# A channel shuffle on one core: where the small tile stands, and the last stores in halves

## Chip, core and metric

The kernel runs on one core of a Trainium2 chip. The metric is the device time of one execution in microseconds (us); lower is better.

## The reference

The input is a float32 tensor of 16 x 64 x 64 x 256 (67.1 MB). Each row of 256 channels is seen as 8 groups of 32; the two are transposed inside the row.

```python
x = x.reshape(batch, h, w, groups, channels_per_group)   # 8 groups of 32
x = x.transpose(0, 1, 2, 4, 3)
x = x.reshape(batch, h, w, c)
```

Nothing is computed. Every byte must be read once and written once: 134.2 MB in all.

## The kernel before

The 65,536 rows are cut into tiles. A tile of size q gives each of the 128 partitions q rows of 1 KB, which are contiguous in memory. So a tile of 24 is "24 KB per partition", 3 MB in all, and one load or store of it is 128 runs of 24 KB.

```python
_SIZES = [24] * 20 + [8, 24]      # rows of 1 KB per partition; sum 512
_BUFS = 8
_PIECE = 8
# ...
    for q in _SIZES:
        buf = pool.tile([P, biggest * c], F32, name="buf")
        nc.sync.dma_start(out=buf[:, : q * c], in_=rows(x_flat, first, q))
        for k in range(0, q, _PIECE):
            piece = buf[:, k * c : (k + _PIECE) * c]
            bounce = psum.tile([P, _PIECE * c], F32, name="bounce")
            nc.vector.tensor_copy(          # the shuffle, SBUF to PSUM
                out=bounce.rearrange("p (i j g) -> p i j g", j=CPG, g=G),
                in_=piece.rearrange("p (i g j) -> p i j g", g=G, j=CPG),
            )
            nc.scalar.copy(out=piece, in_=bounce)   # and back
        nc.scalar.dma_start(out=rows(out_flat, first, q), in_=buf[:, : q * c])
        first += P * q
```

SyncE (SP) issues the loads, VectorE (DVE) shuffles pieces of 8 KB into PSUM, ScalarE (ACT) copies them back over the piece, and ScalarE also issues the stores. Loads and stores share eight completion semaphores in turn (the trace shows eight numbers for all 44 DMAs). Before the change, each of the 36 DMAs that reuse one was issued only after the DMA that used it last had landed, 6 of them within 0.1 us. So the order of all DMAs, and not only buffers, decides who waits for whom.

## Time and profile before

| | before |
|---|---|
| time, median of the first 3 runs (317.38 to 317.92) | 317.67 us |
| span of the profile | 315.9 us |
| load queue and store queue, share of the 16 DMA engines' span | 49.9% + 49.4% |
| VectorE, ScalarE busy | 72%, 38% |
| last store: issue, landing | 302.46 us, 12.4 us later |

The first lines are from the profile page of the kernel before: the span, the rows of 40 slices (busy tenths of VectorE, ScalarE and the DMA engines, then GB/s), the two DMA queues (q1 loads, q10 stores) with packets, MB and share of 16 engines, and the chain of waits by engine.

```profile
span 315.9 us, 289 instructions
...
DVE  0699999959587685957008986999970299999900
ACT  0354455525252424330015416545500444555420
...
DMA  8999999999999999999999999999999999999997
GB/s 296 439 442 380 436 429 433 433 439 433 423 442 433 426 442 426 426 442 426 433 436 427 433 436 436 433 426 437 433 423 448 423 429 444 429 423 433 439 432 302
...
q1 hardware_dynamic: 3168, 67.11, 49.9%
q10 hardware_dynamic: 3168, 67.11, 49.4%
...
DVE 54%; another core or an unknown queue 23%; issue 8%; ACT 5%; DMA 3%; DVEq 1%; ACTq 0%
```

Read the DMA row first: 9 in 38 slices of 40, and the two queues together fill 99.3% of the engines' span. VectorE has two holes (0 in the middle, 02 near three quarters) that leave no mark in the DMA row. The chain of waits names VectorE for 54%. It follows releases backwards from the last instruction and does not know that a released DMA had to queue behind others.

These lines are from the timeline of the kernel before (start, duration, engine, line, operation): the start, one of the stops, and the end. ACTq is ScalarE's sequencer issuing a store, SPq is SyncE issuing loads.

```profile
0.73 3.06 SPq L50 DMA_DIRECT2D buf<-in_x_dram  x6
11.05 3.60 DVE L54 COPY bounce<-buf 128x2048 f32<-128x2048 f32 x1 [11.05 <-DMA buf<-in_x_dram]
...
248.38 0.34 ACTq L59 DMA_DIRECT2D out_dram<-buf  x1
248.81 3.63 ACT L58 COPY buf<-bounce 128x2048 f32<-128x2048 f32 x2 [19.19 <-DMA buf<-in_x_dram]
250.71 3.65 DVE L54 COPY bounce<-buf 128x2048 f32<-128x2048 f32 x1 [15.93 <-ACT buf L58]
...
297.01 1.86 ACT L58 COPY buf<-bounce 128x2048 f32<-128x2048 f32 x1 [1.69 <-DVE bounce L54]
300.57 1.86 ACT L58 COPY buf<-bounce 128x2048 f32<-128x2048 f32 x1 [1.69 <-DVE bounce L54]
302.46 0.34 ACTq L59 DMA_DIRECT2D out_dram<-buf  x1
```

Near 248 us ScalarE could not issue a store, because the semaphore it was to reuse belonged to a load that had not landed (by the semaphore records it landed at 248.3 us; the store went out at 248.38). Its copies stood behind that store for 19.19 us, and VectorE stood behind ScalarE for 15.93 us. The DMA engines had other work queued (from 220 to 252 us they moved 434 GB/s, at a busy share of 1.01), so this cost nothing.

The trace also has a record of every packet: start, duration, bytes, queue. A 24 KB packet takes 912 ns, an 8 KB packet 309 ns, a semaphore write 9 ns (medians). The page counts 16 DMA engines, and from 10 to 300 us 16 records were in progress for 93% of the time and 17 for nearly all of the rest, so I count each record on one of 16 engines.

### The profile page before, as it was taken

The page shows a single profiled execution, that of the slowest core. Times are in us where ns is not written, and L with a number is a line of the kernel's source. Part 1 is how long each engine was busy: PE and PEld are TensorE (multiplying, and loading weights), DVE is VectorE, ACT ScalarE, POOL GpSimd, SP SyncE. Part 2 cuts the span into 40 slices and gives each one's busy share as a digit, 9 for nine tenths or more (in the row PEclk, how much of TensorE's full clock was granted, in tenths as well). Part 3 has the DMA queues.
Part 4 walks back from the last instruction along what each step waited for, and adds up shares of the span by engine and source line. Part 5 has one row for each costly group of instructions (what it writes and reads, how often), then busy time and mean ns, then how long its engine had stood idle before and what let it go on. Part 6 is the DMA issues. An engine that isn't in the chain of part 4 may idle for free.

```text
span 315.9 us, 289 instructions
## 1 busy us (share of the span) xinstructions
DVE 227.9 (72%) x64; ACT 120.3 (38%) x65; POOL 0.2 (0%) x4
## 2 busy tenths in 40 slices
DVE  0699999959587685957008986999970299999900
ACT  0354455525252424330015416545500444555420
POOL 0000000000000000000000000000000000000000
DMA  8999999999999999999999999999999999999997
GB/s 296 439 442 380 436 429 433 433 439 433 423 442 433 426 442 426 426 442 426 433 436 427 433 436 436 433 426 437 433 423 448 423 429 444 429 423 433 439 432 302
DMA packets 6338, 134.24 MB, mean 425 GB/s; under 512 B 704, under 2 KB 704, under 8 KB 704
## 3 DMA queue, kind: packets, MB, share of 16 engines
q1 hardware_dynamic: 3168, 67.11, 49.9%
q10 hardware_dynamic: 3168, 67.11, 49.4%
q14 instruction: 2, 0.02, 0.0%
HBM read 67.11 MB, written 67.11 MB: 425 GB/s over the span
## 4 chain that ended last, share of the span: by engine, by line
DVE 54%; another core or an unknown queue 23%; issue 8%; ACT 5%; DMA 3%; DVEq 1%; ACTq 0%
DVE bounce L54 54%; ACT buf L58 5%; DMA buf<-in_x_dram 3%; DVEq L91 1%; ACTq L59 0%; DVEq L54 0%; ACTq L58 0%
## 5 line engine op out<-in xcount | busy, mean ns | idle before, releaser
L54 DVE COPY bounce<-buf 128x2048 f32<-128x2048 f32 x64 | 227.9, 3636 | 72.6 <-ACT buf L58 38.8
L58 ACT COPY buf<-bounce 128x2048 f32<-128x2048 f32 x64 | 119.0, 1866 | 171.1 <-DVE bounce L54 115.3
L58 ACT ACT_TABLE_LOAD x1 | 1.3, 1283 | 11.1 <-DMA buf<-in_x_dram 11.1
L77 POOL MEMSET const-bfloat16-1.0<- 128x1 bf16 x1 | 0.1, 102 | 0.0
L77 POOL MEMSET const-uint8-127<- 128x1 uint8 x1 | 0.1, 101 | 0.0
L77 POOL MEMSET const-float32-0.0<- 128x1 f32 x1 | 0.1, 99 | 0.2 <-issue 0.2
L77 POOL MEMSET const-float32-1.0<- 128x1 f32 x1 | 0.1, 98 | 0.0
## 6 DMA issues: line engine op xcount, KB each, us to landing
buf<-in_x_dram SPq DMA_DIRECT2D x21, 3072.0 KB, 58.4
out_dram<-buf ACTq DMA_DIRECT2D x21, 3072.0 KB, 24.2
buf<-in_x_dram SPq DMA_DIRECT2D x1, 1024.0 KB, 46.0
out_dram<-buf ACTq DMA_DIRECT2D x1, 1024.0 KB, 15.8
```

The costliest lines, as they stand in the source:

```text
L54: nc.vector.tensor_copy(out=bounce.rearrange("p (i j g) -> p i j g", j=CPG, g=G), in_=piece.rearrange("p (i g j) -> p i j g", g=G, j=CPG),)
L58: nc.scalar.copy(out=piece, in_=bounce)
L77: nc = _bacc.Bacc("TRN2", target_bir_lowering=False, num_devices=1)
L91: with _tile.TileContext(nc) as tc:
```

## The change

The intent: let VectorE start earlier by loading the 8 KB tile first, and give the end of the program finer stores. This makes 48 DMAs of 44.

```diff
-_SIZES = [24] * 20 + [8, 24]
+_SIZES = [8] + [24] * 21
...
+_HALVED = (18, 19, 20, 21)
...
-    for q in _SIZES:
+    for t, q in enumerate(_SIZES):
...
-        nc.scalar.dma_start(out=rows(out_flat, first, q), in_=buf[:, : q * c])
+        n = 2 if t in _HALVED else 1
+        for k in range(n):
+            cols = slice(k * q // n * c, (k + 1) * q // n * c)
+            nc.scalar.dma_start(
+                out=rows(out_flat, first, q)[:, cols], in_=buf[:, cols]
+            )
```

## The prediction

> **What bounds the kernel now.** The DMA engines. The queue table gives loads 49.9% and stores 49.4% of the 16 DMA engines' span of 315.9 us, 99.3% together; the slice row shows DMA at 9 in 38 of 40 slices, 425 GB/s over the span. [...] this trace's 24 KB packets take 912 ns each on one of 16 engines, 431 GB/s[...]. VectorE is 72% busy, ScalarE 38%. The chain of waits shows 54% VectorE, which misleads: the last store is issued at 302.46 us and lands 12.4 us later, although its own eight packets per engine need 7.3. It queues about 4 us behind earlier stores, so the engines don't run dry at the end.
>
> Budget per DMA engine: 336 packets of 24 KB x 0.912 + 16 of 8 KB x 0.309 + 44 semaphore writes x 0.009 = 311.8 us. First packet at 1.7 us, about 0.6 of slow first packets, 0.5 of stagger at the end: last packet at 314.6. Then 1.3 to the span's end, 1.8 more to the timed 317.67.
>
> **What the change does.**
> - Bytes, VectorE copies (64 x 3.64 us) and ScalarE copies (64 x 1.87): the same.
> - 8 KB tile first: VectorE's first copy starts near 6-7 us instead of 11.05, as the first landing needs a third of the bytes. But the DMA engines are full of loads then; an earlier first store only changes the mix. Worth 0.
> - The end: the last tile's stage is the same three VectorE pieces, 3.55 us apart. Worth 0.
> - Halves: ScalarE's order keeps all three copies of a tile ahead of both its stores, so the first half starts no earlier. Four more issues (0.34 us each, off the path); 32 packets of 24 KB per engine become 64 of 12 KB. From 309 ns for 8 KB and 912 for 24 KB I estimate 460 for 12 KB: 32 x 7.5 + 4 x 9 ns = +0.3 us.
> - Eight completion semaphores are shared by loads and stores in turn, so 48 DMAs shift who waits for whose landing (before: ScalarE's store near 248 us waited for a load, stopping VectorE 16 us). Stepping the new order through with the durations above (estimate), stalls move, several transfers stay queued throughout, and the last half store is issued near 301.7 us with some 5 us of earlier work ahead: never dry.
>
> [...]
>
> **Prediction: 317.9 us**, range 317.2 to 318.8. Faster by over 2%: 0.01; within 2%: 0.98; slower: 0.01.
>
> **What would show it.** Both queues again sum to 99%; DMA slices 9 throughout; first VectorE copy at 6-7 us; VectorE and ScalarE busy unchanged; span within 0.6 us of 315.9; eight half stores of 1536 KB, the last two issued within 0.4 us of each other near 302 us; ScalarE's waits for load landings in other places, but not at the very end.
>
> **What would make it wrong.** If semaphore sharing delays the last stores by over 4 us, the engines run dry and each further us counts fully. If 12 KB packets are slower than 460 ns, or half rows write slower, 1 us or more. If small first packets shorten the slow start, up to 0.6 us gained.

311.8 us of packets per engine, the first packet, slow packets, stagger and ends up to the timed 317.67, and 0.3 us for the halves come to 318.0; the forecast put it at 317.9.

## The result, and the profile after

| | before | after |
|---|---|---|
| time, median of 6 runs each | 317.63 us (317.38 to 317.92) | 317.57 us (317.47 to 317.98) |
| ratio, 95% interval | | 1.0 (0.9987 to 1.0013) |
| span | 315.9 us | 315.7 us |
| first VectorE copy | 11.05 us | 5.62 us |
| last store issued (after: its halves) | 302.46 us | 298.81 and 300.64 us |

A ratio here is the mean time of one kernel's fast runs over the mean of the other's fast runs of the same rounds, so it is not quite the ratio of the quoted medians.

The same lines of the page of the kernel after:

```profile
span 315.7 us, 295 instructions
...
DVE  2599979595959577695956049999904999999800
ACT  1245552442425252424330044555204554445500
...
DMA  7999999999999999999999999999999999999997
GB/s 317 403 414 409 442 445 420 433 445 436 414 445 439 411 445 442 408 445 445 406 442 445 408 442 445 420 436 442 431 420 442 436 420 439 439 417 423 433 430 330
...
q1 hardware_dynamic: 3168, 67.11, 49.8%
q10 hardware_dynamic: 3744, 67.11, 49.5%
...
DVE 45%; another core or an unknown queue 22%; DMA 14%; issue 6%; ACT 5%; DVEq 1%; SPq 1%; ACTq 1%
```

VectorE's row has moved: it starts in the first slice, and its holes stand elsewhere. The chain of waits has changed from 54% to 45% VectorE. The DMA row is still 9 between its outer slices and the queues sum to 99.3%. By this reading the DMA row sets the time; the experiments below test it.

The timeline of the kernel after, at its start, near 280 us and at its end:

```profile
5.62 3.60 DVE L56 COPY bounce<-buf 128x2048 f32<-128x2048 f32 x1 [5.62 <-DMA buf<-in_x_dram]
...
13.10 3.60 DVE L56 COPY bounce<-buf 128x2048 f32<-128x2048 f32 x1 [3.88 <-DMA buf<-in_x_dram]
...
276.48 1.87 ACT L60 COPY buf<-bounce 128x2048 f32<-128x2048 f32 x1 [1.69 <-DVE bounce L56]
276.54 5.92 ACTq L64 DMA_DIRECT2D out_dram<-buf  x2
282.50 3.63 ACT L60 COPY buf<-bounce 128x2048 f32<-128x2048 f32 x2 [4.16 <-DMA buf<-in_x_dram]
...
298.75 1.87 ACT L60 COPY buf<-bounce 128x2048 f32<-128x2048 f32 x1 [1.69 <-DVE bounce L56]
298.81 2.17 ACTq L64 DMA_DIRECT2D out_dram<-buf  x2
```

There are two things to see. VectorE starts early, but then waits 3.88 us for the second load. And at 298.81 the first half store is issued 0.06 us after the tile's last copy *started*, not after it ended: the first half needs only the first two pieces, and ScalarE's sequencer issued the DMA while the copy ran. These two pieces had been copied by 297.06 us already (the copy before started at 295.19 and took 1.87); what still held the half store was the third copy, which stands before it in ScalarE's order and had not started. (Three other tiles are stored in halves in this trace; their first halves were issued at 265.89, 276.54 and 288.15 us, each 0.06 or 0.07 us after the start of the tile's last copy.) The second half follows when that copy is done, 1.83 us later (the "x2" line merges the two: 2.17 us less the 0.34 us of one issue).

### The sum of the packets

To see differences far below 1% I added up the packet records of each trace, as a mean of the 16 DMA engines (sums over all packets, divided by 16). "Nominal" is every packet at the usual duration of its size. "Slow" is what packets took beyond that, before and after the change nearly all in the first 30 us. The records do not name the engine, so the other two are counted over all 16 together: "overlap" is the records in progress beyond 16 at a time, and "idle" is what is missing from 16, at the start (before 10 us), in between, and at the end (after 300 us). An engine that idles while another's records overlap would not be seen. Nominal + slow - overlap + idle is the time of the last packet, to within rounding of 0.01. All in us. The lower rows are experiments that follow. Each row is one profiled execution, and the runs of one kernel differ by 0.5 us and more, so tenths in this table describe that execution.

| kernel | DMAs | nominal | slow | overlap | idle start | idle between | idle end | last packet |
|---|---|---|---|---|---|---|---|---|
| before | 44 | 311.77 | 1.77 | 1.44 | 1.88 | 0.04 | 0.55 | 314.56 |
| after | 48 | 312.06 | 1.50 | 1.55 | 2.12 | 0.03 | 0.43 | 314.60 |
| small tile first alone | 44 | 311.77 | 1.43 | 1.44 | 2.17 | 0.06 | 0.29 | 314.28 |
| halves alone | 48 | 312.07 | 1.68 | 1.56 | 1.87 | 0.04 | 0.58 | 314.67 |
| all stores halved | 65 | 313.31 | 1.47 | 2.06 | 2.14 | 0.03 | 0.51 | 315.40 |
| 8 KB packets | 44 | 316.81 | 1.48 | 3.32 | 2.43 | 0.03 | 0.63 | 318.07 |
| 16, ten of 48, 16 | 24 | 310.17 | 1.97 | 0.71 | 2.05 | 0.04 | 0.97 | 314.49 |
| 8, ten of 48, 24 in halves | 26 | 310.31 | 1.67 | 0.76 | 2.11 | 0.04 | 0.48 | 313.85 |
| before, last tile late | 44 | 311.77 | 1.70 | 1.43 | 1.91 | 0.03 | 7.57 | 321.55 |
| small tile first, last tile late | 44 | 311.77 | 1.75 | 1.43 | 1.88 | 0.04 | 4.70 | 318.71 |
| after, last tile late | 48 | 312.06 | 1.49 | 1.54 | 2.13 | 0.04 | 4.11 | 318.29 |
| all stores in quarters | 107 | 316.37 | 7.73 | 3.13 | 2.35 | 7.16 | 10.27 | 340.76 |

Before and after differ by 0.29 in nominal, by 0.1 in overlap, and by 0.1 to 0.3 in the rest. "Idle between" is 0.04 of 290 us: the 16 engines together never run dry between 10 and 300 us.

### The profile page after: what moved, and what is told of

It is laid out like the page before. It is cut to its first block, busy times and chain, and to the rows that moved or that the text cites. A ratio compares the mean times of both kernels' runs of the same rounds, so it can differ in the third digit from the quotient of the medians.

```text
span 315.7 us, 295 instructions
## 1 busy us (share of the span) xinstructions
DVE 228.0 (72%) x64; ACT 120.3 (38%) x65; POOL 0.2 (0%) x4
## 4 chain that ended last, share of the span: by engine, by line
DVE 45%; another core or an unknown queue 22%; DMA 14%; issue 6%; ACT 5%; DVEq 1%; SPq 1%; ACTq 1%
DVE bounce L56 45%; DMA buf<-in_x_dram 14%; ACT buf L60 5%; DVEq L98 1%; SPq L52 1%; ACTq L64 1%; DVEq L56 0%; ACTq L60 0%
```

## The experiments

The theory (A): the 16 DMA engines are the only limit, they do not run dry until the last store, and time is the sum of packet times plus fixed ends. The rivals: (B, C) the two parts of the change have real effects that cancel; (S) the shared semaphores are a second limit.

### The two parts alone

```diff
 small tile first:
-_SIZES = [24] * 20 + [8, 24]
+_SIZES = [8] + [24] * 21
 halves alone (sizes as before; the 8 KB tile is one of the four last):
-        nc.scalar.dma_start(... whole tile ...)
+        two dma_start for tiles 18 to 21, as in the change
```

> The first part of the change alone: the 8 KB tile first, all 22 stores whole. Theory A (the DMA engines are the only limit and never run dry between their first and last packet; time is the sum of packet times plus fixed ends): same packets as before, so 317.6 us within 0.4; first VectorE copy near 5.6 us instead of 11.05, both queues again at 99% together, and at most about 0.3 us gained from quicker first packets. Rival B (the two parts have real effects that cancel in the change: the early small tile gains a microsecond or more by earlier compute, the halves lose as much): this kernel is 1 us or more faster than before, below 316.6 us. Rival C (the small tile first loses, because VectorE then waits longer for the second tile, and the halves win it back): 318.6 us or more.

> The second part alone: sizes as before (8 KB tile last but one), the last four stores in two halves each. Theory A: 32 packets per engine become 64 smaller ones at 7.5 ns more per pair, +0.3 us: 317.9 us within 0.4. Rival B: 318.6 us or more. Rival C: 316.6 us or less, since the last half store has only half the bytes and the first half is issued some 1.8 us earlier.

Measured, five rounds on one chip: small tile first 317.58 us (ratio 0.9995, 0.9983 to 1.0007), halves alone 317.58 us (ratio 0.9995, same interval). Each part alone does nothing that the runs can tell from zero. B and C, which need effects of 1 us or more, are out. The packet sums say a little more, from one profile each. A small first load does not shorten the start in sum: slow and idle at the start together are 3.65 us before, 3.60 with the small tile first, and 3.62 in the changed kernel. (The packets of the first 3 us are less slow, 0.38 us with the small tile first against 0.92, but the idle time at the start is 0.29 us longer and the packets from 10 to 30 us are 0.2 slower.) Its last packet is 0.28 us sooner (314.28 against 314.56) only because the engines happened to end more evenly (0.29 against 0.55). The halves alone end 0.11 us later (314.67).

### More packets: all stores in halves

```diff
-_HALVED = (18, 19, 20, 21)
+_HALVED = tuple(range(1, 22))
```

> The changed kernel with all 21 stores of 24 KB in two halves (65 DMAs). Doubles up the suspected cost of splitting. Theory A with an additive cost per packet: per engine 136 more split packets than the change has, 136 x 7.5 ns + 17 x 9 ns = +1.2 us against the changed kernel: about 318.8 us, within 0.4, DMA still at 99%. If packets cost nothing of their own: 317.6. If the 8 shared completion semaphores run short with 65 DMAs: VectorE and ScalarE stop longer, the DMA slices show gaps below 9 near the end, and the time is 320 us or more.

Measured: 318.66 us (318.23 to 319.70), ratio 1.004 (1.0024 to 1.0055); the expected 318.8 holds. In the packet sums the nominal part grows by 1.25 against the change, as expected, but overlap takes 0.51 of it back. So a packet more costs less than its record says. VectorE stood behind ScalarE for 68.2 us here (38.8 before), and the DMA row still shows 9, with 0.03 us idle between 10 and 300 us: the longer stops alone did not make the engines run dry. The timed difference is larger than the profile's 0.8 us (315.40 against 314.60); two of the six runs were at 319.6 and 319.7, and why is open.

### Fewer packets: tiles of 48 KB

```diff
-_SIZES = [8] + [24] * 21
-_BUFS = 8
+_SIZES = [16] + [48] * 10 + [16]
+_BUFS = 4
-_HALVED = (18, 19, 20, 21)
+_HALVED = ()
```

> Fewer and larger packets: tiles 16, then ten of 48 KB, then 16, in 4 buffers (the same 192 KB per partition), stores whole, 24 DMAs. Theory A with an additive cost per packet of 7.5 ns: 160 packets of 48 KB and 32 of 16 KB per engine instead of 352: saves 160 x 7.5 ns + 20 x 9 ns = 1.4 us: about 316.3 us, within 0.5, provided the last stores still find the DMA engines with work queued. If a packet of 48 KB is split or runs at a lower rate: no gain, 317.6. If fewer, larger tiles let the engines run dry at the end (the last 48 KB tile takes VectorE 21 us): a gap in the last slices and 318 us or more.

Measured: 317.54 us, but from 316.64 to 319.77; ratio 1.0009 (0.9984 to 1.0035). The expected 316.3 was missed. A 48 KB packet takes 1815 ns, 9 ns less than two of 24 KB, so the nominal part is 1.6 us shorter. Overlap is 0.73 smaller, and the engines end less evenly: idle at the end is 0.97 instead of 0.55. Slow packets and idle at the start add 0.37. In the profiled run 0.07 us is left. The wide spread of the runs is not explained.

### The last tile late: how much slack the end has

Three redundant VectorE copies of the last tile's first piece make the last store about 10.7 us later, in the kernel before, in the one with the small tile first, and in the changed one. The result stays correct.

```diff
+            for _ in range(1 + (3 if t == 21 and k == 0 else 0)):
-            nc.vector.tensor_copy(...)
+                nc.vector.tensor_copy(...)
```

> The kernel before, with three redundant VectorE copies (the same piece again) in the last tile, so that its last store is issued 10.7 us later. Measures how far the end is from running dry. Theory A: the DMA engines have other stores until about 306.7 us[...], so an issue up to 305.5 us costs nothing; before issued at 302.46, so 3.0 us are free and the other 7.7 are paid: 325.3 us within 1. If the last store is instead on the critical path already (as the chain of waits seems to say): the full +10.7, 328.3 us.

> The same three redundant copies on the kernel with the 8 KB tile first and whole stores. Its last store was issued at 299.6 us, so 5.9 us are free and 4.8 are paid: 322.4 us within 1. If the place of the small tile did nothing even to the slack: as the kernel before with the same delay, about 325.3.

> The same three redundant copies on the changed kernel. Its first half store was issued at 298.8 us and the second at 300.6. Theory A: the first half needs to be issued by 305.5, so 6.7 us are free and about 4.0 are paid: 321.6 us within 1, some 3.7 below the kernel before with the same delay: both parts of the change buy slack at the end, which the unchanged program does not need. If the halves add nothing: as with the small tile alone, about 322.4.

| last tile late | last store issued, in time / late | time | over the 317.58 us of before in the same rounds | delay that cost nothing |
|---|---|---|---|---|
| before | 302.46 / 313.22 us | 324.83 us, ratio 1.0228 | 7.25 us | 10.76 - 7.25 = 3.5 us |
| small tile first | 299.58 / 310.38 us | 322.13 us, ratio 1.0145 | 4.55 us | 10.80 - 4.55 = 6.3 us |
| after (first half) | 298.81 / 309.86 us | 321.15 us, ratio 1.011 | 3.57 us | 11.05 - 3.57 = 7.5 us |

All three came within 0.5 us of what was expected. The limit of 305.5 us in these texts is 306.7 less 1.2 us that I assumed from a store's issue to its first packet; no run had shown this term. The three late traces show 0.84 us (before: 313.22 to 314.06). The page of the kernel before with the late tile, its DMA row and its throughput; then, from its timeline, its last store:

```profile
DMA  8999999999999999999999999999999999999817
GB/s 314 429 426 387 438 438 435 438 438 432 414 423 438 438 438 435 438 435 420 420 432 439 435 435 438 438 421 423 429 438 435 435 417 443 435 438 438 385 50 341
```

```profile
304.22 1.87 ACT L59 COPY buf<-bounce 128x2048 f32<-128x2048 f32 x1 [12.59 <-DVE bounce L55]
...
311.32 1.87 ACT L59 COPY buf<-bounce 128x2048 f32<-128x2048 f32 x1 [1.68 <-DVE bounce L55]
313.22 0.34 ACTq L60 DMA_DIRECT2D out_dram<-buf  x1
```

And the DMA row of the changed kernel with the late tile, with its last stores from the timeline:

```profile
DMA  8999999999999999999999999999999999999948
```

```profile
309.80 1.87 ACT L61 COPY buf<-bounce 128x2048 f32<-128x2048 f32 x1 [1.68 <-DVE bounce L57]
309.86 2.17 ACTq L65 DMA_DIRECT2D out_dram<-buf  x2
```

Now a hole stands in the DMA row ("1", 50 GB/s), the delay beyond the slack shows in the time, and the change matters: with a late last tile it is 3.7 us faster than the kernel before. The small tile first gives 2.7 of these and the halves, added to it, 1.0. So the change does what it was meant to do. It shortens a stage that, in the unchanged program, has 3.5 us of slack already.

### Many more DMAs: all stores in quarters

```diff
-_HALVED = (18, 19, 20, 21)
+_HALVED = tuple(range(1, 22))
-        n = 2 if t in _HALVED else 1
+        n = 4 if t in _HALVED else 1
```

> The changed kernel with all 21 stores of 24 KB in four quarters each (107 DMAs on the same eight completion semaphores). Theory A with packet cost alone: 168 packets of 24 KB per engine become 672 of 6 KB; at 4 ns net each, as the runs so far give, about +2 us: 319.7 us. Theory S (the order of DMAs on eight shared semaphores is a real second limit that the change does not reach): stores wait for landings of other DMAs, ScalarE and with it VectorE stop during the middle, and the VectorE work left over at the end leaves the DMA engines dry: DMA slices below 9 from about 280 us on, VectorE continuous there, 328 us or more.

Measured: 341.44 us, ratio 1.0762 (1.0723 to 1.0801). What theory S expected is seen here, and the loss lies within its "328 or more". The profiled execution was the slowest of the four (343.8 us). The page's rows of VectorE, ScalarE and the DMA engines in this kernel:

```profile
DVE  3599839914708338577592094939576689999980
ACT  1254244304105042416240153332416055555450
...
DMA  7999999999999999999999999999999986886668
```

From its list of waits (who waited for whom, total us, times, longest), two lines of its timeline, and the loads in its page's list of DMA issues (the last figure is the median time from issue to landing):

```profile
ACT buf L60 <- DMA out_dram<-buf: 137.1, 13, 19.1
DVE bounce L56 <- ACT buf L60: 94.8, 13, 15.9
```

```profile
263.62 9.58 ACTq L64 DMA_DIRECT2D out_dram<-buf  x4
273.24 3.63 ACT L60 COPY buf<-bounce 128x2048 f32<-128x2048 f32 x2 [7.81 <-DMA out_dram<-buf]
...
buf<-in_x_dram SPq DMA_DIRECT2D x21, 3072.0 KB, 14.8
```

ScalarE's copies stood 137.1 us behind stores that waited for other landings, and VectorE stood 94.8 us behind ScalarE. (The list puts all of it down to stores. By the semaphore records 26 stores went out just after the last DMA on their semaphore had landed: 19 times it was a store, 7 times a load, as in the line at 263.62, where a load landed at 272.8 and the last quarter went out at 272.9.) The loads had little queue left: 14.8 us from issue to landing, against 60.0 in the changed kernel. The work left over ran at VectorE's pace at the end (99999 in its row), and the DMA engines fell to 6 and 8: 17.0 us idle after 270 us, 0.4 between 10 and 270. Of the 26.2 us by which the last packet is later than in the changed kernel, idle time is 17.2, slow packets are 6.2 (loads of 24 KB took 944 ns in the mean instead of 912; their cause is open), and nominal less overlap is 2.7.

### Packets alone: padding

Quarters change the number of DMAs and the packet size together. Here the 44 DMAs, their order and their semaphores are as before, but 64 bytes of padding between the three pieces of a buffer break each 24 KB run into three of 8 KB.

```diff
-        buf = pool.tile([P, biggest * c], F32, name="buf")
-        nc.sync.dma_start(out=buf[:, : q * c], in_=rows(x_flat, first, q))
+        buf = pool.tile([P, biggest // _PIECE, _PIECE * c + 16], F32, name="buf")
+        n = q // _PIECE
+        nc.sync.dma_start(
+            out=buf[:, :n, : _PIECE * c],
+            in_=rows(x_flat, first, q).rearrange("p (n f) -> p n f", n=n),
+        )
 ... and the store in the same way
```

> The cost of a packet by itself: the kernel before with the same 44 DMAs, order and semaphores, but 64 B of padding between the three 8 KB pieces of a buffer, so that every load and store of 24 KB per partition goes as three runs of 8 KB. Per engine 1024 packets of 8 KB instead of 336 of 24 KB and 16 of 8 KB: 672 more. If a packet costs its measured 7.5 ns more: +5.0 us, 322.7. If neighbouring packets overlap as the earlier runs showed (about 3.5 ns for each packet, so 4 ns net): +2.7 us, 320.3 within 0.8. Theory S for the quarter stores (it was the order of semaphores, not the packets, that cost 24 us): DMA stays at 9 in the slices here, and VectorE's stops stay where they were before. If small packets were the cause there: far more than 323 us here.

Measured: 321.05 us, ratio 1.0104 (1.0089 to 1.012), within the expected 320.3 +- 0.8. The page's rows of VectorE and DMA and its queues:

```profile
DVE  0599999959577594956008987999960399999900
...
DMA  7999999999999999999999999999999999999997
...
q1 hardware_dynamic: 8544, 67.11, 50.1%
q10 hardware_dynamic: 8544, 67.11, 49.6%
```

There are 2.7 times the packets, VectorE's holes are where they were before, and the DMA row stays at 9. The last packet is 3.51 us later (318.07 less 314.56) for 672 more packets per engine: 5.2 ns each. Of that, nominal less overlap is (5.04 - 1.88) / 672 = 4.7 ns. So packet size costs a per cent and leaves the engines fed. It does not explain the 24 us of the quarters; those have 6 KB packets, not 8, and only in the stores, but the idle engines and the stores' waits are what the padding does not bring. Whether the number of DMAs or their order on eight semaphores is what counts was not separated.

### A version from the parts

The experiments say what may help a little: fewer packets (with 48 KB the nominal part was 310.17 us instead of 311.77), and finer stores at the end so that the larger packets do not end unevenly (idle at the end was 0.97 us there and 0.43 in the changed kernel).

```diff
-_SIZES = [8] + [24] * 21
-_BUFS = 8
+_SIZES = [8] + [48] * 10 + [24]
+_BUFS = 4
-_HALVED = (18, 19, 20, 21)
+_HALVED = (10, 11)
```

> A version built from the parts: 8 KB tile first, ten tiles of 48 KB, one of 24 KB last, 4 buffers, the last two stores in two halves each (26 DMAs). The packet sum is 1.6 us less than before, of which the overlap takes 0.7 back; quicker first packets give 0.25; halves keep the end from being coarser than before. Theory A: about 316.8 us, 0.3% less than before, a difference at the limit of what five rounds tell. If 48 KB packets lose at the ends what they save, as with the 16, 48, 16 tiles: 317.5. If the engines run dry before the last store: 318.5 or more.

Measured: 316.82 us (316.78 to 316.88) against 317.61, ratio 0.9972 (0.9959 to 0.9984). The expected 316.8 holds, and the interval excludes 1: 0.3% less than before. It is small, since the packets at their usual durations are 310 of the 317 us. In the packet sums the last packet is 0.71 us sooner: nominal less overlap gives 0.78 of that, and the rest moves by a tenth. Its text credited 0.25 us to quicker first packets; slow and idle at the start are 3.78 us here against 3.65 before, so in the sum that part is not there.

## Why the prediction was right

317.9 us (317.2 to 318.8) was predicted, 317.57 measured. The forecast "within 2%" and its reason held: the bound is the DMA engines, at 99.3% before and after, and nothing that the change moves lies on it.

Point by point:

- **The bound.** Shown: "idle between" is 0.04 us or less in before and after, and when the engines are made to run dry the time follows (7.25 us for a delay of 10.76).
- **Small tile first, worth 0.** Right within what the runs tell: ratio 0.9995. VectorE's first copy came at 5.62 us, earlier than the 6 to 7 predicted. The prediction allowed "up to 0.6 us gained" from the slow start under what would make it wrong; the packets of the first 3 us did lose 0.5 us of slowness (0.92 to 0.42), but a longer idle start and slower packets up to 30 us took it back, so that the sum stayed within 0.05 us.
- **Halves, +0.3 us.** The mechanism was right: 12 KB packets took 460 ns as estimated, and nominal grew by 0.29. The term was mis-sized, because overlap gives about 0.1 back; a further packet costs 5 ns and not 7.5 (padding). The two kernels' last packets differ by 0.04 us instead of 0.3: +0.29 nominal, -0.11 overlap, and -0.12 because the engines ended a little more evenly, which one profile cannot tell from chance.
- **"The first half starts no earlier."** Wrong. It was issued 1.83 us before the second, while the tile's last copy ran. The order of instructions on ScalarE was read as an order of completions; the half store waited for the third copy to start (298.75) and not to end. It changed nothing here, as the engines had other stores queued; with a late tile it is part of the 1.0 us that the halves gave. "Within 0.4 us of each other" fell with it. The last half went out at 300.64 us, where 301.7 was stepped through.
- **Semaphores.** The stops moved, as predicted (15.93 us on VectorE near 250 before; 11.61 near 240 after). One did come rather late: near 277 us a second half store went out 5.2 us after the end of the first half's issue, because a load on its semaphore landed only at 282.0 us; its own copy had been done for 3.8 of these. It was harmless: from 276 to 284 us the engines moved 436 GB/s. That stores waiting for semaphores can leave the engines dry is seen in the quarters (17.0 us idle after 270 us), far from this change.
- **"Over about 4 us" of slack.** Measured 3.5 us before; the change raised it to 7.5.

How much could another order of tiles have won? The 24 KB packets here come to 24,576 B / 912 ns x 16 = 431 GB/s and the 48 KB ones (1815 ns) to 433. At 433 GB/s, the higher of these two measured rates, the 134.2 MB would take 309.8 us; with the 1.9 us of idle start and the 3.1 us from the last packet to the timed end that are measured here it is 314.8 us, 0.9% less than 317.6. This is an estimate from these packet durations and leaves overlap out (0.71 us with 48 KB packets). By it no order of tiles with packets of these sizes could have won 2%. Splitting the last four stores gained only once the last tile was made late and the engines idled: 1.0 us there, and nothing that the runs can tell from zero without the delay (halves alone: ratio 0.9995).

## What to carry to other kernels

When two DMA queues sum to 99% of the engines and the throughput between the ends is that of the packets (here 380 to 448 GB/s in the inner slices, where 24 KB packets come to 431), look at earlier starts, finer stores and shorter waits as slack and not as time: ask how late the last store may be before the engines run dry, and measure it by making it late. The chain of waits can name a compute engine for half the span in such a kernel (VectorE 54% here); the sum of packet records says better what is left, and here that was packet count and the two ends (0.78 us of packets less overlap in the version from the parts; 3.65 us slow and idle at the start and 0.55 idle at the end before). Do not split DMAs without counting them: with eight shared completion semaphores, four times as many stores cost 24 us where packets of a third of the size cost 3.4. Whether their number or their order made the difference is open.
